# Second FFN's early u weights in tiles of their own, a scaling moved to ScalarE, and S5 output tables built in the latents' S5 projection

## The chip, the cores and the metric

The kernel runs on one core of a Trainium2 chip. The metric is the device time of one execution in microseconds (us), as the median of several executions; less is better. Engines: PE is TensorE, PEld its weight load, DVE is VectorE, ACT is ScalarE, POOL is GpSimd, SP is SyncE, whose queue issues nearly all of the DMAs here.

## What is computed

One layer of a diffusion backbone over 1024 latent tokens of width 1024, with 256 context tokens beside them, all in float32:

```
x   = x   + 0.5*gate *rms_norm((silu(g)*u) @ w_down)     # first FFN, g,u = split(h @ w_gu)
ctx = the same FFN on the context tokens
p   = modulate(rms_norm(x)) @ w_in -> bg, cg, v, u       # context: only u
y_conv = bg * grid_short_conv(cg * v)
states = S5 scan of u in both directions, from the context's last states
y_ssm  = gelu(Re(C states) + d*u), times a sigmoid gate (GLU)
x   = x + mod * rms_norm(concat(y_conv, y_ssm) @ w_out)
x   = x + 0.5*gate2*rms_norm((silu(g)*u) @ w_down2)      # second FFN
```

The FFN's inner width is 2816. Here h is the normed, modulated input. Every S5 group of 16 channels has 64 complex states; 8 neighbouring tokens form one step of the scan, so that powers 0 to 8 of the state's multiplier and tables made from them and from B and C are needed.

## The kernel before

**Stages, in order of time in the profile.** First FFN on the latents, up projection (`g_lat`, to about 540 us), first FFN on the context (`g_ctx`, to about 705 us), the down projections of both (`d_ctx`, `d_lat`, to about 1005 us), the latents' and the context's S5 input projections (`u_lat`, `u_ctx`, to about 1075 us), the S5 pairs beside the conv branch (`s5_pair`, `conv`, to about 1250 us), the output projection with the GLU (to about 1380 us), the second FFN's up projection (`g_lat` again, to about 1875 us) and its down projection.

**Matmuls.** A product is made of three passes on a high and a low half (fp32r) of both operands; `split` makes the halves with a ScalarE copy and a VectorE subtraction. The latents' FFN uses Strassen's scheme of seven products m = 1 to 7 for each of 22 feature tiles f. The first 16 products of `g_lat` (the list `early`: m = 1, 2, 5, 3 for f = 0 to 3) are an exception: they multiply raw float32, which the profile shows as two passes per matmul, 8 for a product, so that they need no halves. For m = 1 and 2 the operand is a slice of the g weights, for m = 5 it is u0+u1, for m = 3 it is g1-(u0+u1-g0); `prep` makes these on VectorE, one and three operations of 128x512.

**Weights.** Weight tiles of 512 KB pass through four buffers `wr0` to `wr3`. At build time `g_lat` simulates which tile sits in which buffer and writes a list `loads`; an entry is issued (`fetch`) once the last use of its buffer's previous tile has been emitted. With g and u of four feature tiles there are eight tiles for four buffers, so that in the second FFN u tiles replace g tiles, and g tiles come back:

```
slots, loads = [None] * 4, []
...
if n == len(early) and not apart_u:
    slots = [None] * 4
```

With `apart_u=True`, which the first FFN's call passes and the second's does not, the u tiles that the early products need are loaded by `u_load` into tiles of the pool z (32 buffers of 512 KB, shared by nearly everything), the four g tiles stay in their buffers, and the slots are not emptied after the early products.

**Order.** The framework's scheduler orders the instructions of each engine at build time: by priority (order of emission) among those that its simulation holds to be ready, and it gives out pool buffers in the same way. In the first FFN's start the program fixes the order on VectorE and TensorE (`G0`), later not. `S2` is the order in which hop steps (`h`: transposed, modulated input blocks, their Strassen sums and halves) and products (`p`) are emitted at the second FFN's start. Its m = 6 sums overwrite the tiles that m = 5's raw products read; the m = 3 products read the tiles that m = 6 frees.

**S5 tables.** `s5_prep` runs as filler of `g_ctx` (`step(FC)`, two filler steps for each feature tile). Its last loop makes the output tables, columns `CO` of `pd` in DRAM: for 4 blocks of 8 groups, six operations of 128x1024 each (24 in all), those of odd blocks on POOL and of even blocks on VectorE, and two stores of 512 KB for each block on SP's queue. `s5_pair` loads its rows of `pd` (`self.load(pa, self.pd[a, :, :EO])`) one pair ahead; the first such load is behind `u_ctx`.

**Projections.** `u_lat` is called for two halves and yields ten times in all; between its steps `run` advances `ctx_in`, the norm of the context.

Of the kernel before, what the change touches and what calls it, by code (L numbers as in the profile page):

```python
# [16 lines left out]
P = 128  # L17
D = 1024
# [8 lines left out]
H = 16  # L27
T8 = 8
# [40 lines left out]
class Kernel:  # L69
# [111 lines left out]
    def setup(self):  # L181
        nc, i = self.nc, self.i
        self.cp = self.pool("cp")
        self.dr = self.pool("dr", space=bass.MemoryType.DRAM)
        self.psum = self.pool("psum", bufs=8, space=bass.MemoryType.PSUM)
        self.sm = self.pool("sm", bufs=8)
        self.wp = self.pool("wp", bufs=6)
        self.tp = self.pool("tp", bufs=1)
        self.tb = self.t(self.tp, [P, 5 * D], "tb")
        self.ring([self.tb[:, D * k : D * k + D] for k in range(5)])  # L190
        self.wrs = [self.t(self.wp, [P, D], f"wr{k}", bufs=1) for k in range(4)]
        self.zp = self.pool("zp", bufs=32)

        dr = self.dr
        self.x1d = self.t(dr, [T8, CL, D], "x1d")
        self.x2d = self.t(dr, [T8, CL, D], "x2d")
        self.rowd = [self.t(dr, [KT, P], f"rowd{k}") for k in range(4)]
        self.pd = self.t(dr, [PAIRS, P, TO], "pd")
        self.pwd = self.t(dr, [P, D], "pwd")
        self.brd = self.t(dr, [P, D], "brd")  # L200
        self.gd = self.t(dr, [H, G, 15, H], "gd")
        self.td = self.t(dr, [P, G, P], "td")
        self.ud = self.t(dr, [G * H, T8, CL], "ud")
        self.ucd = self.t(dr, [G * H, T8, CC], "ucd")
        self.yd = self.t(dr, [T8, H, G, CL], "yd")
        self.zd = [self.t(dr, [P, NT], f"zd{k}") for k in range(4)]
        self.t1d = [self.t(dr, [P, 512], f"t1d{k}") for k in range(NF // 2)]
        self.t2d = [self.t(dr, [P, 512], f"t2d{k}") for k in range(NF // 2)]
        self.scd = [self.t(dr, [P, 4 * NC], f"scd{k}") for k in range(6)]
        self.sd = [[self.t(dr, [P, NT], f"sd{n}_{k}") for k in range(NF)] for n in range(2)]  # L210

        cp = self.cp
        rows = self.t2([16, P])
        self.load(rows[0:8, :], i["c"][0].rearrange("(k p) -> k p", p=P))
        self.load(rows[8:16, :], i["c_ctx"].rearrange("(k p) -> k p", p=P))
        self.ident = self.t(cp, [P, P], "ident")
        make_identity(self.tc.nc, self.ident)
        srow = self.t2([16, P])
        nc.scalar.activation(srow, rows, AF.Silu)
        pt = self.ps()  # L220
        self.tr(pt[:, :16], srow, 16)
        self.scol = self.t(cp, [P, 16], "scol")
        nc.vector.tensor_copy(self.scol, pt[:, :16])
        self.srep = self.t(cp, [P, KT, 32], "srep")
        nc.scalar.activation(
            self.srep.rearrange("p k (n c) -> p n c k", c=2),
            pt[:, :16].rearrange("p (c k) -> p c k", c=2).unsqueeze(1).to_broadcast([P, 16, 2, KT]), AF.Copy,
        )
        self.ones = self.t(cp, [P, 1], "ones")
        nc.gpsimd.memset(self.ones, 1.0)  # L230
        self.modc = {}
        self.mask = self.t(cp, [P, 2 * CL + 4], "mask", dt=mybir.dt.bfloat16)
        nc.gpsimd.memset(self.mask, 1.0)
        nc.gpsimd.memset(self.mask[:, :: CL + 1], 0.0)
# [1147 lines left out]
    def s5_prep(self):  # L1382
        nc, i = self.nc, self.i
        pl = nc.gpsimd
        slot = lambda shape: self.t(self.zp, shape, "z")
# [4 lines left out]
        pw, br_ = slot([P, 2, 2, T8, 32]), slot([P, 2, 32, H])  # L1390
# [4 lines left out]
        ct = slot([P, 2, 32, H])  # L1395
# [4 lines left out]
        for k in range(2):  # L1400
# [4 lines left out]
            for d in range(2):  # L1405
                r = slice(64 * d, 64 * d + 64)
# [3 lines left out]
        pdv = self.pd.rearrange("a p w -> p a w")  # L1410
        shp = [P, 8, T8, H]

        def power(w, r, gs):
            return pw[:, w, r, :, gs].rearrange("p t a -> p a t").unsqueeze(3).to_broadcast(shp)

        for o in range(4):
            gs = slice(8 * o, 8 * o + 8)
            xr, xi, xt = slot(shp), slot(shp), slot(shp)
# [38 lines left out]
        for t in range(T8):  # L1457
            r = slice(t * H, t * H + H)
# [6 lines left out]
        for t in range(T8):  # L1465
            r = slice(t * H, t * H + H)
            self.load(self.td[r], self.gd[:, :, 7 - t : 15 - t].rearrange("h g l k -> h g (l k)"))
            if t % TY == TY - 1:
                yield
        for o in range(4):  # L1470
            gs = slice(8 * o, 8 * o + 8)
            mr, mi, xt = slot(shp), slot(shp), slot(shp)
            prb, pib = power(1, 0, gs), power(1, 1, gs)
            cr_ = ct[:, 0, gs, :].unsqueeze(2).to_broadcast(shp)
            ci_ = ct[:, 1, gs, :].unsqueeze(2).to_broadcast(shp)
            e = pl if o % 2 else None
            self.mul(mr, cr_, prb, e)
            self.mul(xt, ci_, pib, e)
            self.add(mr, mr, xt, e)
            yield  # L1480
            self.mul(mi, ci_, prb, e)
            self.mul(xt, cr_, pib, e)
            self.sub(mi, mi, xt, e)
            for r, m in ((0, mr), (1, mi)):
                c0 = CO + 256 * r
                self.load(
                    pdv[:, 4 * o : 4 * o + 4, c0 : c0 + 256], m.rearrange("p (a q) t h -> p a (q t h)", q=2)
                )
            yield
# [225 lines left out]
    def run(self):  # L1715
        nc, i = self.nc, self.i
# [10 lines left out]
        hb = {m: [] for m in range(1, 8)}  # L1727
        hr = {m: [] for m in (1, 2, 5, 3)}
        xt = [self.z() for _ in range(4)]
# [8 lines left out]
        held = {f: {1: halves(tb[f])[0], 2: halves(tb[f])[1], 0: [tb[f]]} for f in range(4)}  # L1738
        held[0][5], held[0][3] = halves(tb[4])
        held[0][0].append(tb[4])  # L1740
        ffn = self.g_lat(i["ffn1_w_gu"][0], hb, hr, self.sd[0], FN, order1, 3, held, True)
# [18 lines left out]
        ab = (self.modc[1, 0], self.modc[0, 0])  # L1760
# [7 lines left out]
        bl = [self.blocks(xt, *ab), self.blocks(xt2, *ab)]  # L1768
        h = self.hops(stages, bl, hb, hr)
# [145 lines left out]
        u = self.tb.rearrange("p (g c) -> p g c", g=G)  # L1915
        cx = ctx_in()
        next(cx)
        for _ in itertools.chain(self.u_lat(mhi, mlo, 0, u), self.u_lat(mhi, mlo, 1, u)):
            next(cx, None)
        for _ in cx:  # L1920
            pass
        self.u_ctx(chi2, clo2)
# [100 lines left out]
        order2 = [(f, m) for m in (1, 2, 5, 3) for f in range(4)]  # L2023
        tb = [self.ta() for _ in range(3)]
        held = {f: {1: halves(tb[f])[0], 2: halves(tb[f])[1], 0: [tb[f]]} for f in range(3)}
        ffn = self.g_lat(i["ffn2_w_gu"][0], hb, hr, self.sd[1], (0, 0, 1, 1, 0, 1, 0), order2, 3, held)
        next(ffn)
        for _ in range(4):
            self.g_fetch()
# [10 lines left out]
        ss.append(spl(3))  # L2040
        acc = self.out_group(ss[2], wo2)
        next(p)
        ssa = self.squares(part[:4])
        for _ in range(4):
            self.g_prep()
# [15 lines left out]
        self.eager = True  # L2061
        for _ in range(4):
            self.g_prod(4, 8)
        bl[1] = self.normer(part[4:], ssa, *ab)
        for _ in range(4):
            self.g_prod(4, 99)
        act = dict(h=lambda: next(h), p=lambda: self.g_prod(4, 99))
# [106 lines left out]
```

## Time and profile before

| | |
|---|---|
| median of 3 runs (lowest to highest) | 2077.2 us (2076.4 to 2079.46) |
| the profiled execution, its span | 2077.89 us, 2076.1 us |
| mean granted TensorE clock | 0.98 |
| HBM | 282.97 MB read, 74.17 MB written |
| DMA issues for w_gu through the four buffers | 146 of 512 KB, median 4.1 us to landing |

The span is the part of the execution in which the profile has instructions; 1.8 us lie around it. In the views below all lines of the kernel read L51, the helper that records each instruction, so that groups are told apart by tile names: `ps` are PSUM banks, `wr` the raw weight buffers, `w` weight halves, `z` and `t` the two large pools.

### The profile page before, as it was taken

The page shows a single profiled execution, that of the slowest core. Times are in us where ns is not written, and L with a number is a line of the kernel's source. Part 1 is how long each engine was busy: PE and PEld are TensorE (multiplying, and loading weights), DVE is VectorE, ACT ScalarE, POOL GpSimd, SP SyncE. Part 2 cuts the span into 40 slices and gives each one's busy share as a digit, 9 for nine tenths or more (in the row PEclk, how much of TensorE's full clock was granted, in tenths as well). Part 3 has the DMA queues.
Part 4 walks back from the last instruction along what each step waited for, and adds up shares of the span by engine and source line. Part 5 has one row for each costly group of instructions (what it writes and reads, how often), then busy time and mean ns, then how long its engine had stood idle before and what let it go on. Part 6 is the DMA issues. An engine that isn't in the chain of part 4 may idle for free. (4 is left out here: it accounts for less than half of the span.)

```text
span 2076.1 us, 25812 instructions
## 1 busy us (share of the span) xinstructions
PE 1961.8 (94%) x9364; PEld 1562.7 (75%) x9364; DVE 1433.3 (69%) x2532; ACT 825.3 (40%) x1459; POOL 191.3 (9%) x106
## 2 busy tenths in 40 slices
PE   7899999989898999999998899997999999999997
PEld 3477778867898877777887778763788888887775
DVE  1874469787766679787528985486865555577977
ACT  5433333423343345566532334353333333334543
POOL 0000000040347000000003430010000000000000
PEclk9999999999999999999999999999999999999999
DMA  9167632445579977476665533134632322267554
GB/s 325 31 218 249 240 137 72 132 127 167 172 222 268 294 249 251 147 259 224 180 207 170 182 112 122 53 130 122 203 122 81 100 73 82 87 254 267 198 182 162
DMA packets 334059, 356.78 MB, mean 172 GB/s; under 512 B 47024, under 2 KB 248428, under 8 KB 333932
## 3 DMA queue, kind: packets, MB, share of 16 engines
q1 hardware_dynamic: 331628, 346.75, 51.4%
q10 hardware_dynamic: 2304, 8.39, 1.0%
q8 instruction: 73, 1.20, 0.2%
q14 instruction: 54, 0.44, 0.1%
HBM read 282.97 MB, written 74.17 MB: 172 GB/s over the span
## 5 line engine op out<-in xcount | busy, mean ns | idle before, releaser
L51 PE MATMUL ps<-z,w 128*128 128x512 f32 (+1 forms) x5328 | 1151.2, 377 | 39.6 <-DVE w L51 13.1
L51 PEld LDWEIGHTS ps<-z,w 128*128 128x128 f32 x5328 | 937.7, 192 | 236.4 <-DVE w L51 14.9
L51 PE MATMUL ps<-w,w 128*128 128x512 f32 x1848 | 427.3, 392 | 16.3 <-DVE w L51 9.7
L51 PEld LDWEIGHTS ps<-w,w 128*128 128x128 f32 x1848 | 346.4, 188 | 95.6 <-DVE w L51 14.7
L51 ACT ACTIVATE w<-wr 128x512 fp32r<-128x512 f32 (+1 forms) x270 | 206.6, 767 | 348.4 <-PE ps L51 281.7
L51 DVE TENSOR_TENSOR w<-wr,w 128x512 fp32r<-128x512 f32 (+1 forms) x264 | 246.9, 937 | 117.4 <-ACT w L51 110.8
L51 ACT ACTIVATE w<-t 128x512 fp32r<-128x512 f32 x292 | 177.1, 626 | 213.4 <-DVE t L51 129.9
L51 DVE TENSOR_TENSOR w<-t,w 128x512 fp32r<-128x512 f32 x292 | 198.6, 691 | 77.0 <-ACT w L51 76.6
L51 DVE TENSOR_TENSOR t<-t,ps 128x512 f32<-128x512 f32 x150 | 102.4, 684 | 97.6 <-PE ps L51 94.5
L51 PE MATMUL ps<-z,t 128*128 128x512 f32 x512 | 148.0, 449 | 11.4 <-DVE t L51 10.3
L51 ACT ACTIVATE t<-ps 128x512 f32<-128x512 f32 (+2 forms) x143 | 77.4, 542 | 166.3 <-PE ps L51 162.8
L51 PEld LDWEIGHTS ps<-z,t 128*128 128x128 f32 x512 | 96.8, 190 | 60.8 <-issue 36.2
L51 ACT ACTIVATE w<-z 128x512 fp32r<-128x512 f32 x110 | 69.6, 632 | 146.2 <-PE ps L51 144.0
L51 DVE TENSOR_TENSOR z<-z,z 128x512 fp32r<-128x512 f32 (+3 forms) x127 | 106.6, 869 | 15.5 <-ACT z L51 11.6
L51 DVE TENSOR_TENSOR t<-wr 128x512 f32<-128x512 f32 x140 | 94.2, 686 | 32.2 <-DMA wr<-in_ffn_w_gu 18.1
L51 ACT ACTIVATE t<-z 128x1024 bf16<-128x1024 f32 (+3 forms) x132 | 75.5, 605 | 47.2 <-DVE z L51 30.8
L51 DVE TENSOR_TENSOR w<-z,w 128x512 fp32r<-128x512 f32 x110 | 75.5, 686 | 26.6 <-ACT w L51 26.4
L51 POOL TENSOR_TENSOR z<-z,z 128x1024 f32<-128x1024 f32 x24 | 79.2, 3320 | 76.3 <-PE ps L51 42.0
L51 ACT ACTIVATE t<-t 128x512 f32<-128x512 f32 (+1 forms) x83 | 51.7, 623 | 78.6 <-DVE t L51 78.2
L51 DVE TENSOR_TENSOR z<-t,ps 128x512 f32<-128x512 f32 (+1 forms) x52 | 29.8, 573 | 64.9 <-PE ps L51 64.3
L51 POOL TENSOR_TENSOR tb<-tb 128x512 f32<-128x512 f32 x24 | 33.6, 1412 | 435.4 <-DMA sd<-z 409.0
L51 ACT ACTIVATE z<-z 128x512 fp32r<-128x512 f32 (+2 forms) x76 | 48.3, 673 | 56.7 <-DVE z L51 56.7
(121 smaller groups left out, 1402.1 us busy)
## 6 DMA issues: line engine op xcount, KB each, us to landing
wr<-in_ffn_w_gu SPq DMA_DIRECT2D x146, 512.0 KB, 4.1
wr<-in_ffn_w_down SPq DMA_DIRECT2D x198, 256.0 KB, 4.2
tb<-in_w_ada SPq DMA_DIRECT2D x56, 512.0 KB, 4.5
sd<-z SPq DMA_DIRECT2D x44, 512.0 KB, 3.0
z<-sd SPq DMA_DIRECT2D x88, 256.0 KB, 5.4
wr<-in_ffn_w_down SPq DMA_DIRECT2D x22, 512.0 KB, 4.9
wr<-in_w_in SPq DMA_DIRECT2D x20, 512.0 KB, 4.0
z<-in_w_ada SPq DMA_DIRECT2D x16, 512.0 KB, 6.3
```

What stands on the lines that cost most here:

```text
L51: r = f(*a, **kw)
```

## The change

Three parts. (1) The output tables leave `s5_prep`: it now stores the transposed C table `ct` to a new DRAM tensor `ctd`; a new generator `s5_ctab` loads the half of `pwd` with the powers and `ctd`, and makes the same four blocks, all on VectorE; `run` advances it one step after each yield of `u_lat`. (2) The second FFN's `g_lat` gets `apart_u=True`, and four `u_load` calls are put behind the second residual block's `next(p)`. (3) The scaling of the second half of the rows (`part[4:]`) by its norm runs on ScalarE; only this use of `normer` is replaced.

```diff
@@ -198,6 +198,7 @@
         self.pd = self.t(dr, [PAIRS, P, TO], "pd")
         self.pwd = self.t(dr, [P, D], "pwd")
         self.brd = self.t(dr, [P, D], "brd")
+        self.ctd = self.t(dr, [P, D], "ctd")
         self.gd = self.t(dr, [H, G, 15, H], "gd")
         self.td = self.t(dr, [P, G, P], "td")
         self.ud = self.t(dr, [G * H, T8, CL], "ud")
@@ -1467,20 +1468,30 @@
             self.load(self.td[r], self.gd[:, :, 7 - t : 15 - t].rearrange("h g l k -> h g (l k)"))
             if t % TY == TY - 1:
                 yield
+        self.load(self.ctd, ct.rearrange("p r a h -> p (r a h)"))
+
+    def s5_ctab(self):
+
+        slot = lambda shape: self.t(self.zp, shape, "z")
+        pw, ct = slot([P, 2, T8, 32]), slot([P, 2, 32, H])
+        self.load(pw.rearrange("p r t a -> p (r t a)"), self.pwd[:, 512:])
+        self.load(ct.rearrange("p r a h -> p (r a h)"), self.ctd)
+        pdv = self.pd.rearrange("a p w -> p a w")
+        shp = [P, 8, T8, H]
+        yield
         for o in range(4):
             gs = slice(8 * o, 8 * o + 8)
             mr, mi, xt = slot(shp), slot(shp), slot(shp)
-            prb, pib = power(1, 0, gs), power(1, 1, gs)
+            prb, pib = (pw[:, r, :, gs].rearrange("p t a -> p a t").unsqueeze(3).to_broadcast(shp) for r in range(2))
             cr_ = ct[:, 0, gs, :].unsqueeze(2).to_broadcast(shp)
             ci_ = ct[:, 1, gs, :].unsqueeze(2).to_broadcast(shp)
-            e = pl if o % 2 else None
-            self.mul(mr, cr_, prb, e)
-            self.mul(xt, ci_, pib, e)
-            self.add(mr, mr, xt, e)
-            yield
-            self.mul(mi, ci_, prb, e)
-            self.mul(xt, cr_, pib, e)
-            self.sub(mi, mi, xt, e)
+            self.mul(mr, cr_, prb)
+            self.mul(xt, ci_, pib)
+            self.add(mr, mr, xt)
+            yield
+            self.mul(mi, ci_, prb)
+            self.mul(xt, cr_, pib)
+            self.sub(mi, mi, xt)
             for r, m in ((0, mr), (1, mi)):
                 c0 = CO + 256 * r
                 self.load(
@@ -1915,8 +1926,12 @@
         u = self.tb.rearrange("p (g c) -> p g c", g=G)
         cx = ctx_in()
         next(cx)
+        ctab = self.s5_ctab()
         for _ in itertools.chain(self.u_lat(mhi, mlo, 0, u), self.u_lat(mhi, mlo, 1, u)):
             next(cx, None)
+            next(ctab, None)
+        for _ in ctab:
+            pass
         for _ in cx:
             pass
         self.u_ctx(chi2, clo2)
@@ -2023,7 +2038,7 @@
         order2 = [(f, m) for m in (1, 2, 5, 3) for f in range(4)]
         tb = [self.ta() for _ in range(3)]
         held = {f: {1: halves(tb[f])[0], 2: halves(tb[f])[1], 0: [tb[f]]} for f in range(3)}
-        ffn = self.g_lat(i["ffn2_w_gu"][0], hb, hr, self.sd[1], (0, 0, 1, 1, 0, 1, 0), order2, 3, held)
+        ffn = self.g_lat(i["ffn2_w_gu"][0], hb, hr, self.sd[1], (0, 0, 1, 1, 0, 1, 0), order2, 3, held, True)
         next(ffn)
         for _ in range(4):
             self.g_fetch()
@@ -2040,6 +2055,8 @@
         ss.append(spl(3))
         acc = self.out_group(ss[2], wo2)
         next(p)
+        for _ in range(4):
+            self.u_load()
         ssa = self.squares(part[:4])
         for _ in range(4):
             self.g_prep()
@@ -2061,7 +2078,8 @@
         self.eager = True
         for _ in range(4):
             self.g_prod(4, 8)
-        bl[1] = self.normer(part[4:], ssa, *ab)
+        self.scale(part[4:], self.rsq(ssa), nc.scalar)
+        bl[1] = self.blocks(part[4:], *ab)
         for _ in range(4):
             self.g_prod(4, 99)
         act = dict(h=lambda: next(h), p=lambda: self.g_prod(4, 99))
```

## Rows read from the trace of the kernel before

**Rows 1.** The page, part 1: busy time and share of each engine.

```profile
PE 1961.8 (94%) x9364; PEld 1562.7 (75%) x9364; DVE 1433.3 (69%) x2532; ACT 825.3 (40%) x1459; POOL 191.3 (9%) x106
```

**Rows 2.** Windows: length, then busy time and count by engine, PEclk, DMA share, GB/s.

```profile
640.00:700.00 60.00, 47.62 (x356) 45.90 (x355) 44.41 (x36) 17.22 (x24) 36.51 (x8) 0.91 0.91 268
...
1408.24:1456.31 48.07, 34.76 (x99) 16.33 (x97) 37.29 (x62) 17.58 (x31) 0.00 (x0) 0.92 0.38 110
1005.00:1062.00 57.00, 56.01 (x286) 46.76 (x284) 21.79 (x40) 24.74 (x46) 2.44 (x1) 1.00 0.61 177
...
1080.00:1250.00 170.00, 153.86 (x775) 130.17 (x774) 145.56 (x337) 52.13 (x117) 61.12 (x41) 0.95 0.49 163
...
1396.00:1408.24 12.24, 12.24 (x29) 5.27 (x28) 4.92 (x9) 1.89 (x3) 0.00 (x0) 1.00 0.36 112
```

**Rows 3.** Groups of instructions, 640 to 700 us: busy us, mean ns | idle before, releasers.

```profile
L51 PE MATMUL ps<-z,w 128*128 128x256 f32 x356 | 48.0, 297 | 12.4 <-ACT w L51 6.8 <-DVE w L51 5.5
...
L51 POOL TENSOR_TENSOR z<-z,z 128x1024 f32<-128x1024 f32 x8 | 36.5, 4593 | 1.2 <-DMA scd<-z 1.1
L51 DVE TENSOR_TENSOR w<-wr,w 128x1024 fp32r<-128x1024 f32 x15 | 23.4, 1578 | 8.2 <-ACT w L51 8.1
L51 DVE TENSOR_TENSOR z<-z,z 128x1024 f32<-128x1024 f32 x12 | 17.7, 1513 | 0.0
```

**Rows 4.** Timeline of PE, 667 to 693 us: start, us, instruction [idle before <-releaser].

```profile
667.32 4.42 PE L51 MATMUL ps<-z,w 128*128 128x256 f32 x24 [1.67 <-ACT w L51]
672.18 3.11 PE L51 MATMUL ps<-z,w 128*128 128x256 f32 x24 [0.45 <-DVE w L51]
678.46 14.27 PE L51 MATMUL ps<-z,w 128*128 128x256 f32 x118 [3.17 <-DVE w L51]
```

**Rows 5.** Timeline of SP's queue: start, us, DMAs issued.

```profile
649.89 5.69 SPq L51 DMA_DIRECT2D td<-gd  x8
...
656.02 4.77 SPq L51 DMA_DIRECT2D wr<-in_ffn_w_gu  x3
...
1079.77 1.00 SPq L51 DMA_DIRECT2D z<-pd  x2
```

**Rows 6.** Groups of instructions of DVE, 1005 to 1062 us.

```profile
L51 DVE TENSOR_TENSOR w<-wr,w 128x1024 fp32r<-128x1024 f32 x6 | 7.4, 1226 | 18.5 <-ACT w L51 14.4 <-PE ps L51 4.0
...
L51 DVE TENSOR_TENSOR z<-z,gate 128x1024 f32<-128x1024 f32 x1 | 1.2, 1224 | 1.6 <-ACT t L51 1.6
```

**Rows 7.** DMA issues: queue, count, size, median us to landing.

```profile
pd<-z SPq DMA_DIRECT2D x16, 512.0 KB, 3.8
...
z<-in_ffn_w_gu SPq DMA_DIRECT2D x4, 512.0 KB, 9.5
```

**Rows 8.** Timeline of PE at the second FFN's start.

```profile
1412.88 17.51 PE L51 MATMUL ps<-z,t 128*128 128x512 f32 x40 [0.98 <-DVE t L51]
...
1437.56 5.72 PE L51 MATMUL ps<-z,t 128*128 128x512 f32 x8 [7.16 <-DVE t L51]
...
1456.31 13.88 PE L51 MATMUL ps<-z,w 128*128 128x512 f32 x47 [1.61 <-DVE w L51]
```

**Rows 9.** Groups of instructions of DVE, 1408.24 to 1456.31 us.

```profile
L51 DVE TENSOR_TENSOR t<-wr 128x512 f32<-128x512 f32 x10 | 6.6, 688 | 9.5 <-DMA wr<-in_ffn_w_gu 9.5
```

**Rows 10.** The chain of waits: start, us, what.

```profile
1456.31 416.93 PE ps L51 x1783
```

**Rows 11.** Timeline of PE at the first FFN's start.

```profile
65.00 27.63 PE L51 MATMUL ps<-z,t 128*128 128x512 f32 x64
99.01 3.66 PE L51 MATMUL ps<-z,w 128*128 128x512 f32 x7 [6.37 <-ACT z L51]
103.34 14.29 PE L51 MATMUL ps<-z,w 128*128 128x512 f32 x53 [0.68 <-DVE z L51]
```

**Rows 12.** Timelines: the scaling of part[4:] on DVE, and an ACT operation of 128x1024.

```profile
1396.27 2.74 DVE L51 TENSOR_SCALAR z<-z,sy 128x1024 f32<-128x1024 f32 x4
...
1390.65 1.06 ACT L51 ACTIVATE t<-z 128x1024 bf16<-128x1024 f32 x1
```

## The prediction

> **What bounds the kernel now.** The page comes first: TensorE is busy for 94% of the span [rows 1], so time can go only where PE is idle or runs at a lower clock, and an operation moved between other engines is worth what it does to PE there. Then the windows [rows 2]. Each of the two stages that lose work holds a hole. From 640 to 700 us PE is busy for 47.6 of 60 us at a granted clock of 0.91, with DVE at 44.4 and POOL at 36.5. From 1408.24 to 1456.31 us it is busy for 34.8 of 48.1 us at 0.92, with DVE at 37.3. The projection stage, which takes the tables over, has PE busy for 56.0 of 57 us: nothing to win, but cover for other engines, since DVE works there for 21.8 us only. Third, groups and timelines of the two holes.
>
> In the first, PE waits 12.4 us in all, 5.5 for DVE's weight halves and 6.8 for ScalarE's [rows 3]. The tables are on DVE and POOL at that time: 12 DVE operations of 17.7 us, and 8 POOL operations of 36.5 us, 4.6 each. DVE's 15 weight subtractions take 1578 ns each beside them, 1226 where POOL rests [rows 3, 6]. The longest PE wait, 3.17 us, ends with such a subtraction [rows 4].
>
> In the second, PE waits 7.16 us before the sixth of the eight late early-products (m = 5 and 3) [rows 8], and DVE itself waited 9.5 us for w_gu transfers [rows 9]: u tiles can be fetched only when a g tile's last reader is through. After 1456.31 us PE runs 1783 matmuls without a wait that enters the chain [rows 10], so a gain made before it should arrive at the end.
>
> **The change, part by part.**
>
> *Tables out of the context's FFN.* This removes 24 operations and 8 stores there and adds one store of 512 KB. The waits for DVE's halves, 5.5 us, go. The clock lost behind them: 24 matmuls took 4.42 us in one place and 3.11 in the next [rows 4], 1.3 us. The waits for ScalarE, 6.8 us, I leave: they follow weight transfers issued behind eight td transfers that hold SP's queue for 5.7 us [rows 5], and these remain. Their ends are 0 (should the transfers move the stall elsewhere) and 12.4 + 1.3 = 13.7 us; I take 5.5 + 1.3 = 6.8, the part whose cause is removed. What is late next is the weight tile behind the td transfers.
>
> *Tables into the projections.* All 24 operations are now DVE's, at 1224 ns (the same shape, POOL resting [rows 6]): 29.4 us. DVE's idle time in that stage is 57.0 - 21.8 = 35.2 us [rows 2], so PE's projections cover them; with that cover gone they would cost up to 29.4. SP gets 2 loads and 8 stores, POOL loses work and nobody waits for it there. The added wait is a store's for DVE: behind it on SP stand the next weight columns of w_in and the u rows. On DVE six weight subtractions may stand behind three table operations. A block of tables needs six operations and a landed store before its buffers are free, 6 x 1.22 + 3.8 = 11.1 us [rows 7]; four blocks, 45 us, from about 1015 us end near 1060, 20 us ahead of the first pair's load at 1079.77 [rows 5]. The ends are 0 (all in idle time) and two subtractions that each wait for a three-operation step, 2 x 3.7 = 7.4 us; near the lower end, since 29.4 is less than 35.2, I take 1.5.
>
> *u tiles of their own.* No operation is added; fetches before the 9.5 us of waits go, and the four u tiles come through z buffers beforehand. The first FFN's own u tiles land 9.5 us after issue [rows 7], and here some 40 us lie between issue and use. The best case: PE never waits from 1411.9 to 1456 us, so all of 48.07 - 34.76 = 13.3 us go, and the clock stays up: 8 passes took 5.72 us where 64 take 27.63 undisturbed [rows 8, 11], 2.3 us lost; 47 matmuls took 13.88 us where the chain has 416.93 / 1783 = 0.234 each [rows 10], 2.9 us lost. Sum 18.5 us. The lower end is the first FFN, which has this very arrangement: its eight late products (64 passes) run without a gap, yet PE then waits 6.37 us [rows 11], for hop work queued on DVE. From the first of these passes to split products is 99.01 - 65.00 = 34.0 us there, 1456.31 - 1412.88 = 43.4 here [rows 8]: 9.4 better, plus the 0.98 before it, less 3.9 - 2.9 + 0.7 = 1.7 for its slower clock and second gap (60 matmuls in 17.95 us against 14.0), makes 8.7. DVE decides between the two. It has 37.3 us of work in this window. Its 16 preparations for the late products (four for m = 5, twelve for m = 3, 0.69 us each [rows 9], 11.0 us) may move ahead, as far as DVE has room before 1408 us: 12.24 - 4.92 = 7.3 us idle [rows 2], and 2.7 us that the scaling frees. That leaves 27 to 37 us, against 28 us of late products. I take the middle, 13.6: DVE's order is fixed by hand in the first FFN and free here, but it is nearly full.
>
> *Scaling on ScalarE.* Four operations of 1.06 us replace 2.74 us on DVE [rows 12]. They would end near 1400.5 instead of 1399 us, and the transposes that read them wait for PE until 1408.24: 0, hidden by the raw products; without that cover 4.2 - 2.7 = 1.5 us. On DVE it frees room for preparations, which is in the 13.6.
>
> The Trainium skill speaks against this part: "Perfetto Trace Analysis", section Optimizing Scalar/DVE Operations, says that an operation which has a fast mode on DVE is faster there, and that offloading it makes sense if DVE is saturated. By that rule, with DVE idle from 1400 to 1408 us, the sum would be 1.5 us worse; by the trace the price is hidden.
>
> **Sum.** -6.8 + 1.5 - 13.6 = -18.9 us. The profiled execution took 2077.9 us, 1.8 of it outside the span, and lies 0.7 above the median of the runs, 2077.2. That gives 2059.0 for the profiled kind and **2058.3 us** as a median.
>
> **Rivals.**
>
> *DVE limits the second FFN's start as it does in the first.* For it: DVE's 37.3 us, and [rows 11]. Against: free order there. 2077.2 - 6.8 + 1.5 - 8.7 = 2063.2 us. Chance 0.20.
>
> *The u tiles don't get ahead.* The pool's 32 buffers are full around the output projection, so that u_load waits on SP for a buffer and the change does not do what it says. For it: eight row blocks, sixteen weight and GLU tiles and four z tiles live there at once. Against: the GLU halves are released well before 1376 us. Only the tables' part is left: 2077.2 - 6.8 + 1.5 = 2071.9 us. Chance 0.10.
>
> *The tables run on into the S5 pairs: slower.* The buffers for blocks 3 and 4 come late, because the S5 inputs, the context's halves and the ring hold the rest; the table operations go on past 1079.77 us, where DVE is busy for 145.6 of 170 us [rows 2] and each operation there moves the end, 1.22 us each; the pair loads stand behind the stores on SP. All 24 would give 2077.2 - 6.8 - 8.7 + 29.4 = 2091.1 us. It decides from 13 operations on, since 13 x 1.22 = 15.9 exceeds the 15.5 gained elsewhere. Against: 20 us of slack. Chance 0.10.
>
> *The table work was hidden anyway.* The gaps from 640 to 700 us belong to weight transfers, and the second FFN lies between its two ends: 2077.2 + 1.5 - 13.6 = 2065.1 us. For it: 6.8 us of waits for ScalarE. Against: the 3.17 us gap ends on DVE. Chance 0.10.
>
> A rest of 0.05 has both gains lost in a new order of the scheduler, near 2077.
>
> **How the numbers follow.** My forecast has 0.45. A measurement of this kernel tells about 0.2%, 4.2 us, from no change, so the forecast and three rivals (0.45, 0.20, 0.10, 0.10) count as faster, less 0.02 for their upper tails; no change gets the rest of 0.05 and these tails, 0.07; slower gets 0.10. The best sum is 2077.2 - 13.7 - 18.5 = 2045.0, the worst without a slide into the pairs 2077.2 + 7.4 - 8.7 = 2075.9. The range goes from 2046 to 2074: it leaves out the slide and the rest.
>
> **What would show it.** Right: in the context's FFN no POOL operation after about 610 us and weight subtractions at 1.23 us; 24 table operations of 1.22 us on DVE between 1000 and 1060 us with PE still full; the u tiles' loads issued before 1370 us; the late early-products as one row of 64 passes in about 27.6 us, and less than 3 us of gap behind it. Wrong: table operations beyond the first pair's load, a PE wait for weight halves in the projections, a gap of some 6 us ahead of the m = 6 products, or waits for w_gu still there. If the S5 pairs' stage grows by as much as the two holes shrink, the forecast is wrong in kind.

## The result, and the profile after

The changed kernel takes **2067.17 us** as the median of 4 runs (2066.54 to 2067.38), beside 2078.14 us (2076.4 to 2079.46, 4 runs) for the kernel before: a ratio of 0.9947, 95% interval 0.993 to 0.9964, or 11.0 us. Timed again with the experiments it gave 2064.16 us beside 2076.27, ratio 0.9942 (0.9929 to 0.9956). Forecast were 2058.3 us and 18.9 us. It is faster, and inside the range that was given, but the gain is some 60% of the forecast. The profiled execution took 2066.54 us, with a span of 2064.8.

Part 1 of the page, beside [rows 1]: POOL has lost 45 us, and TensorE's work is what it was.

```profile
PE 1960.7 (95%) x9364; PEld 1561.2 (76%) x9364; DVE 1429.4 (69%) x2540; ACT 828.8 (40%) x1463; POOL 146.0 (7%) x94
```

The windows that answer to [rows 2] (length, then busy time and count by engine, PEclk, DMA share, GB/s; the third begins with the second FFN's transposes, as the one before did):

```profile
640.00:700.00 60.00, 53.13 (x416) 52.32 (x415) 24.53 (x26) 20.44 (x26) 0.00 (x0) 0.94 0.81 232
1005.00:1062.00 57.00, 53.86 (x278) 44.73 (x277) 47.58 (x63) 21.53 (x40) 2.18 (x1) 1.00 0.78 233
1406.41:1452.88 46.47, 39.02 (x122) 20.49 (x120) 41.37 (x69) 20.29 (x36) 0.00 (x0) 0.93 0.15 45
...
1080.00:1250.00 170.00, 153.53 (x773) 129.71 (x772) 145.11 (x337) 51.94 (x117) 61.15 (x41) 0.95 0.49 166
```

In the context's FFN, TensorE works 5.5 us more of 60. In the projections it works 2.2 us less of 57, while VectorE's 21.8 us have become 47.6. The second FFN's start is fuller, but VectorE is nearly full there (41.4 of 46.5 us), and the S5 pairs are as they were.

**The context's FFN.** The groups from 640 to 700 us, beside [rows 3]:

```profile
L51 PE MATMUL ps<-z,w 128*128 128x256 f32 x416 | 53.6, 292 | 6.9 <-ACT w L51 5.3 <-DVE w L51 1.5
...
L51 DVE TENSOR_TENSOR w<-wr,w 128x1024 fp32r<-128x1024 f32 x17 | 20.8, 1224 | 27.8 <-ACT w L51 27.8
```

VectorE's weight subtractions are back at 1224 ns, from 1578, and the waits for them fell from 5.5 to 1.5 us; those for ScalarE fell from 6.8 to 5.3. In [rows 3] POOL's table operations ran beside them, now none does. The Trainium skill's "GPSIMD Engine Reference", section Specifications, says that GpSimd shares its SBUF interfaces with VectorE and contends with instructions that have two SBUF inputs; the 1578 and 1224 ns agree.

What is left is one wait. TensorE's timeline, and then SP's queue, beside [rows 4, 5]:

```profile
664.71 0.50 PE L51 MATMUL ps<-z,w 128*128 128x256 f32 x2 [4.66 <-ACT w L51]
665.97 40.12 PE L51 MATMUL ps<-z,w 128*128 128x256 f32 x310 [0.76 <-DVE w L51]
```

```profile
651.28 5.76 SPq L51 DMA_DIRECT2D td<-gd  x8
657.15 12.55 SPq L51 DMA_DIRECT2D wr<-in_ffn_w_gu  x7
```

The weight tiles for it were issued behind eight td transfers, which held SP's queue for 5.76 us.

**The projections.** TensorE had 1.15 us of waits from 1000 to 1078 us (0.99 and 0.16); now its timeline shows 3.11:

```profile
1035.26 0.30 PE L51 MATMUL ps<-ident,z 128*128 128x128 f32 x1 [1.02 <-DVE z L51]
...
1051.52 1.39 PE L51 MATMUL ps<-z,w 128*128 128x256 f32 x7 [1.48 <-ACT z L51]
1053.52 8.68 PE L51 MATMUL ps<-z,w 128*128 128x256 f32 x67 [0.61 <-DVE z L51]
```

VectorE's timeline shows why: between the context norm's operations of 0.15 us stand table operations (`z<-z,z`), two at a time.

```profile
1012.80 6.91 DVE L51 TENSOR_TENSOR z<-z,z 128x1024 f32<-128x1024 f32 x6 [0.53 <-DMA z<-ctd]
...
1026.64 2.36 DVE L51 TENSOR_TENSOR z<-z,z 128x1024 f32<-128x1024 f32 x2
1028.91 0.15 DVE L51 TENSOR_TENSOR sq<-sq,sv 128x2 f32<-128x2 f32 x1
...
1055.06 1.22 DVE L51 TENSOR_TENSOR z<-z,z 128x1024 f32<-128x1024 f32 x1
```

All 24 lie between 1012.80 and 1056.3 us, 22 us ahead of the first pair's load at 1078.74.

**The second FFN's start.** TensorE's timeline, beside [rows 8]:

```profile
1378.94 27.63 PE L51 MATMUL ps<-z,wr 128*128 128x512 f32 x64
...
1409.90 17.33 PE L51 MATMUL ps<-z,t 128*128 128x512 f32 x40
1432.95 12.36 PE L51 MATMUL ps<-z,t 128*128 128x512 f32 x24 [5.72 <-DVE t L51]
...
1446.07 5.38 PE L51 MATMUL ps<-z,w 128*128 128x512 f32 x22 [0.30 <-ACT w L51]
1452.88 47.37 PE L51 MATMUL ps<-z,w 128*128 128x512 f32 x202 [1.43 <-DVE t L51]
```

The waits of 0.98, 7.16, 2.18, 1.37 and 1.61 us (13.3 in all) became 5.72, 0.30 and 1.43 (7.5). The u tiles are ahead, issued from 1309 to 1316 us, but the products still stop at the same place. VectorE's timeline has the cause:

```profile
1399.81 0.69 DVE L51 TENSOR_TENSOR tb<-tb,ps 128x512 f32<-128x512 f32 x1 [2.65 <-ACT z L51]
1403.24 0.69 DVE L51 TENSOR_TENSOR tb<-tb,ps 128x512 f32<-128x512 f32 x1 [2.74 <-PE ps L51]
1406.68 0.69 DVE L51 TENSOR_TENSOR t<-t,ps 128x512 f32<-128x512 f32 x1 [2.74 <-PE ps L51]
...
1417.09 4.29 DVE L51 TENSOR_TENSOR z<-z,z 128x512 fp32r<-128x512 f32 x7
...
1425.51 0.68 DVE L51 TENSOR_TENSOR t<-z 128x512 f32<-128x512 f32 x1
...
1432.12 0.68 DVE L51 TENSOR_TENSOR t<-wr,t 128x512 f32<-128x512 f32 x1
...
1435.74 0.68 DVE L51 TENSOR_TENSOR t<-wr,t 128x512 f32<-128x512 f32 x1
1441.22 0.69 DVE L51 TENSOR_TENSOR t<-wr 128x512 f32<-128x512 f32 x1 [4.80 <-DMA wr<-in_ffn_w_gu]
```

It stands idle for 8.1 us up to 1406.7, waiting for raw products' results; then come hop operations (`z<-z,z`), and only from 1425.5 the nine preparations for m = 3 of features 1 to 3 (`t<-z`, `t<-t,wr`, `t<-wr,t`). The one that ends at 1432.8 is what TensorE waits for at 1432.95. Only when the second and third of these features' last preparations have read their g tiles does SP issue the next two weight tiles, at 1435.28 and 1436.49, and VectorE waits 4.80 us for them.

**Where the time went, by three marks on TensorE's timeline.** The start of the first down projection (`ps<-w,w`, 128x512) closes the context's FFN; the raw products (`ps<-z,wr`) open the second FFN; the 133rd `ps<-w,w` matmul of its down projection, 33 us behind the first, is the third mark. Each row is one profiled execution; the last column is the difference of the two before it. tab_only and ffn_only have one part of the change each, no_scale has all but the scaling, and prep_early all and one edit more; they are explained below.

| kernel | context's FFN closed | raw products begin | 133rd matmul of the down projection | between the last two |
|---|---|---|---|---|
| before | 711.16 | 1380.77 | 1874.92 | 494.15 |
| ffn_only | 714.28 | 1381.27 | 1866.85 | 485.58 |
| tab_only | 706.16 | 1377.44 | 1872.53 | 495.09 |
| after | 705.93 | 1378.94 | 1864.49 | 485.55 |
| after, second time | 703.28 | 1376.36 | 1860.63 | 484.27 |
| no_scale | 706.06 | 1378.46 | 1866.57 | 488.11 |
| prep_early | 706.43 | 1378.87 | 1860.64 | 481.77 |

Kernels that are the same up to a mark differ there by 2 to 3 us, so means are taken. The five with the tables moved close the context's FFN at 705.6, the two without at 712.7: 7.1 us earlier. At the raw products they are at 1378.0 and 1381.0: 3.0 us are left, so 4.1 were given back on the way, of which the waits of the projections show about 2. The stretch between the last two marks, the second FFN's up projection and 33 us of its down projection, went from 494.6 (before, tab_only) to 485.1 us (both profiles of after, and ffn_only): 9.5 us less. Sum 12.5 us, against 11.0 and 12.1 us between the medians.

A mark carries along what lies before it. Counting TensorE's matmuls (9364 in every trace, in nearly the same order) leaves that out. From the 3200th, near 640 us, to the closing of the context's FFN it is 72.4 and 74.4 us in the two kernels with the old tables and 65.0 to 65.4 in the five: 8.1 us less. From the 5000th to the 5400th, the projections and the start of the first pair, it is 79.1 us in each of the two and 81.4 to 83.9 in the five, 3.1 more in the mean; the longer waits are 2 of these. Ahead of the 3200th matmul, and from the closing to the 5000th, TensorE has nearly the same work in all of them and single profiles differ by up to 3.3 us; there the five are 1.0 and 0.9 us slower in the mean, which is why the marks show less for the tables (3.0) than the counts (5.0).

### The profile page after: what moved, and what is told of

The parts are those of the page before. It is cut to its first block, busy times and chain, and to the rows that moved or that the text cites. A ratio compares the mean times of both kernels' runs of the same rounds, so it can differ in the third digit from the quotient of the medians.

```text
span 2064.8 us, 25793 instructions
## 1 busy us (share of the span) xinstructions
PE 1960.7 (95%) x9364; PEld 1561.2 (76%) x9364; DVE 1429.4 (69%) x2540; ACT 828.8 (40%) x1463; POOL 146.0 (7%) x94
## 5 line engine op out<-in xcount | busy, mean ns | idle before, releaser
L51 DVE TENSOR_TENSOR w<-wr,w 128x512 fp32r<-128x512 f32 (+1 forms) x264 | 239.8, 910 | 124.5 <-ACT w L51 121.8
L51 DVE TENSOR_TENSOR z<-z,z 128x512 fp32r<-128x512 f32 (+3 forms) x139 | 114.8, 859 | 15.8 <-ACT z L51 10.6
L51 DVE TENSOR_TENSOR t<-wr 128x512 f32<-128x512 f32 x132 | 89.0, 686 | 30.3 <-DMA wr<-in_ffn_w_gu 15.2
L51 DVE TENSOR_TENSOR w<-z,w 128x512 fp32r<-128x512 f32 x110 | 75.5, 686 | 20.6 <-ACT w L51 20.4
L51 PE MATMUL ps<-w,t 128*128 128x512 f32 x264 | 64.4, 401 | 1.9 <-DVE w L51 1.3
L51 POOL TENSOR_TENSOR tb<-tb 128x512 f32<-128x512 f32 x24 | 35.2, 1481 | 433.1 <-DMA sd<-z 409.6
```

Source lines behind the costliest of these rows:

```text
L51: r = f(*a, **kw)
```

## The experiments

All were timed in five rounds beside the kernel before (medians 2077.49, 2078.08 and 2076.27 us in the three groups in which they ran); ratios are to that. The first four ran together, the next four, and the last two.

**tab_only** and **ffn_only**: each part of the change alone. The edit of tab_only, to the changed kernel, takes the second FFN's part back; ffn_only is the reverse and has the tables in `s5_prep` as before.

```diff
-        ffn = self.g_lat(i["ffn2_w_gu"][0], hb, hr, self.sd[1], (0, 0, 1, 1, 0, 1, 0), order2, 3, held, True)
+        ffn = self.g_lat(i["ffn2_w_gu"][0], hb, hr, self.sd[1], (0, 0, 1, 1, 0, 1, 0), order2, 3, held)
-        for _ in range(4):
-            self.u_load()
-        self.scale(part[4:], self.rsq(ssa), nc.scalar)
-        bl[1] = self.blocks(part[4:], *ab)
+        bl[1] = self.normer(part[4:], ssa, *ab)
```

> The tables' move alone; the second FFN as in the kernel before. Theory A (what the two traces say): it won 5.2 us in the context's FFN and gave 2.4 of them back in the projections and about 0.5 behind them, so that 1.8 us are left: 2076.3 us against 2078.1, within 1.5 us. Rival B (my forecast's terms): -6.8 + 1.5 = -5.3, 2072.8 us. Under A the waits of PE in the projections (1000 to 1060 us) add up to about 3.1 us, against 1.15 before; under B they stay near 1.2.

> The second FFN's two parts alone (u tiles and scaling); the tables as in the kernel before. Theory A: 8.6 us up to the end of that FFN's up projection and about 0.9 in its down projection, together 9.2 to 9.5: 2068.8 us. Rival B: the forecast's 13.6, 2064.5 us. Rival C: the parts work on each other through the scheduler and don't add up: the sum of this run's gain and of the one with the tables alone differs from 11.0 us by more than 2.

Measured: tab_only 2074.65 us, ratio 0.9981 (0.997 to 0.9991), or 3.9 us; ffn_only 2070.45 us, 0.9967 (0.9954 to 0.998), or 6.9 us. They add up to 10.8: as far as these intervals tell, the parts don't disturb each other. tab_only lies between its two theories in time; its waits in the projections, 2.88 us, are those of theory A. ffn_only gained less in time than either of its theories has, though its stretch between the last two marks is that of after. The 5.72 us wait is there in ffn_only too (at 1435.28), so it has nothing to do with the tables, and the wait behind the td transfers is there in tab_only (4.72 us at 665.05).

**prep_early**: the last four preparations of the second FFN are emitted before the second group's steps.

```diff
+        for _ in range(4):
+            self.g_prep()
         act = dict(h=lambda: next(h), p=lambda: self.g_prod(4, 99))
```

> The changed kernel with the preparations of the four m = 3 products emitted ahead of the hop steps. Theory A: the order of DVE's work is what holds the second FFN at the low end of my bounds; the 64 late passes run as one row of 27.6 us, the 5.72 us gap goes, the next weight tiles are fetched sooner, and the time falls by 5 to 8 us, to 2059 to 2062 us. Rival B: the amount of DVE's work is the limit (37 us in that window); the gap only moves behind the late products, and the time stays within 1.5 us of 2067.2.

2061.59 us, ratio 0.992 (0.9903 to 0.9936). TensorE's timeline:

```profile
1410.96 27.73 PE L51 MATMUL ps<-z,t 128*128 128x512 f32 x64 [0.97 <-DVE z L51]
1439.12 1.25 PE L51 MATMUL ps<-z,w 128*128 128x512 f32 x4 [0.43 <-ACT w L51]
1443.44 56.89 PE L51 MATMUL ps<-z,w 128*128 128x512 f32 x237 [3.07 <-DVE w L51]
```

The 64 passes run as one row, the 5.72 us are gone, and waits of 4.47 us are left, 4.04 of them for VectorE. Between the last two marks it is 481.8 us, 3.4 less than with the change alone, and the three later kernels with this edit have 481.8 to 481.9. The time lies in theory A's range, 4.6 to 5.6 us under after, by its two ratios. So the order of VectorE's work held the 5.72 us: the same work, nine operations put ahead of hop operations, closes that gap. The idle time of VectorE up to 1406.6 us is still there (8.15 us), and all twelve preparations for m = 3 come behind it. Whether the amount of VectorE's work holds the 4.47 us that are left, as rival B says, was not tested.

**no_scale**: the change without the scaling on ScalarE.

```diff
-        self.scale(part[4:], self.rsq(ssa), nc.scalar)
-        bl[1] = self.blocks(part[4:], *ab)
+        bl[1] = self.normer(part[4:], ssa, *ab)
```

> The changed kernel with the scaling of part[4:] on VectorE again, the u tiles and the tables as changed. Theory A (the scaling is hidden on either engine: in the changed kernel its last piece is done at 1400.9 and TensorE first needs the transposed blocks at 1406.4, and VectorE stood idle for some 5.5 us just behind it): 2067.2, within 1 us. Theory B (moving it freed VectorE for the preparations that TensorE waits for): four scalings of 0.69 us come back, 2.7 us slower, 2069.9. Theory C (ScalarE is the slower engine for it, and the blocks are late by its longer time): 1.5 us faster, 2065.7.

2069.1 us, ratio 0.9955 (0.9943 to 0.9967), which overlaps with that of after, 0.9942 (0.9929 to 0.9956); the mark tells it better: 488.1 us between the last two, against 484.3 to 485.7 in five profiles of kernels whose second FFN is that of after. TensorE's timeline, then VectorE's:

```profile
1409.42 17.33 PE L51 MATMUL ps<-z,t 128*128 128x512 f32 x40
1433.63 12.09 PE L51 MATMUL ps<-z,t 128*128 128x512 f32 x24 [6.87 <-DVE t L51]
...
1454.19 46.02 PE L51 MATMUL ps<-z,w 128*128 128x512 f32 x191 [2.88 <-DVE t L51]
```

```profile
1396.12 2.74 DVE L51 TENSOR_SCALAR z<-z,sy 128x1024 f32<-128x1024 f32 x4
...
1406.20 0.69 DVE L51 TENSOR_TENSOR t<-t,ps 128x512 f32<-128x512 f32 x1 [2.75 <-PE ps L51]
...
1432.78 0.70 DVE L51 TENSOR_TENSOR t<-wr,t 128x512 f32<-128x512 f32 x1
```

Theory B has the size, 2.7 us, but not the mechanism. The four scalings go into time in which VectorE would have waited: it is at `t<-t,ps` 27.74 us after the raw products' start in both kernels (1406.20 here, 1406.68 in after). What differs is the order behind that, which the scheduler worked out anew: ahead of the preparation that TensorE waits for (`t<-wr,t` at 1432.78 and 1432.12) stand two more operations of 0.68 us, one of a hop and one for the third feature. That is 1.15 us more of wait there (6.87 against 5.72) and 1.45 at the next (2.88 against 1.43). So the scaling's place is worth about 3 us here, by the order that came with it; no run held the order and moved the scaling alone.

**tab_void**: 20 of the 24 table operations left out.

```diff
             self.mul(mr, cr_, prb)
-            self.mul(xt, ci_, pib)
-            self.add(mr, mr, xt)
             yield
-            self.mul(mi, ci_, prb)
-            self.mul(xt, cr_, pib)
-            self.sub(mi, mi, xt)
-            for r, m in ((0, mr), (1, mi)):
+            for r, m in ((0, mr), (1, mr)):
```

> The changed kernel with 20 of the 24 products and sums of the output tables left out (one product a block, written to both places of its store), so the output is not the reference's; both loads and all eight stores stay. Theory A (what the tables cost in the projections is VectorE's queue, in which the context norm's small operations and the input projections' operands stand between 1.22 us operations): TensorE's waits from 1000 to 1078 fall from 3.1 us to about 1.2 us, as before the change, and the time falls by 2 us, to 2065.2. Theory B (it is the loads and stores, or the place of the yields): the waits stay near 3 us and the time at 2067.2.

2064.61 us, ratio 0.9932 (0.9919 to 0.9944). TensorE's timeline is that of before, with the same two waits (0.99 and 0.16 us):

```profile
1049.47 7.00 PE L51 MATMUL ps<-z,w 128*128 128x256 f32 x56 [0.99 <-ACT z L51]
1056.64 30.87 PE L51 MATMUL ps<-z,w 128*128 128x256 f32 x142 [0.16 <-DVE w L51]
```

From the 5000th to the 5400th matmul it is 79.2 us, as before the change. Theory A: VectorE's queue costs the 2 us of waits; the loads and stores, which are all there, cost nothing. The raw products begin at 1375.25 us, 2.8 earlier than the mean with the tables moved.

**td_act**: the eight td transfers on ScalarE's queue. **both**: td_act and prep_early together. **both_pool**: the same, with the transfers on GpSimd's queue (`self.nc.gpsimd.dma_start` in place of `self.store`).

```diff
-            self.load(self.td[r], self.gd[:, :, 7 - t : 15 - t].rearrange("h g l k -> h g (l k)"))
+            self.store(self.td[r], self.gd[:, :, 7 - t : 15 - t].rearrange("h g l k -> h g (l k)"))
```

> The changed kernel with the eight td transfers issued from ScalarE's queue in place of SP's. Theory A: the 4.66 us wait left in the context's FFN comes from SP's queue, which issues the next weight tiles only after 5.8 us of td issues; it goes, and the time falls by 3 to 5 us, to 2062 to 2064 us. Rival B: the td transfers' own packets keep the DMA engines busy, the weight tiles land as late as before, and the time stays within 1 us of 2067.2. Rival C: ScalarE's halves of the weights wait behind the issues, and it is slower than 2068.2.

> The changed kernel with both further edits that gained when made alone: the eight stores of the block Toeplitz tiles on ScalarE's queue, and the last four preparations of the second FFN ahead of the second group's steps. Theory A (different stages, so the gains add: 5.6 and 5.5 us): 2056.1, within 1.5 us. Theory B (part of the gain of one was the clock granted to the whole run, which the other takes too): 2059 to 2061.

> The two edits together, with the eight stores of the block Toeplitz tiles on GpSimd's queue, which has no work from 593 to 1002 us in the changed kernel, in place of ScalarE's. On ScalarE their issue took 9.53 us in front of its own operand copies and left TensorE a wait of 7.01 us at 662.84. Theory A (the wait is the place behind the issuing of the stores, on whichever queue the copies or their weights stand): it goes, but for the 0.7 to 1.2 us waits that the other feature tiles have too, and the time falls by 4 to 6 us under the same kernel with ScalarE's queue, to 2053 to 2055. Theory B (the transfers themselves, 2 MB that compete with the weights, make the operands late): a wait of 4 to 7 us stays, and the time is 2059 within 1.5 us.

td_act gave 2061.72 us, ratio 0.9923 (0.9905 to 0.9942), about the time that was expected; its trace does not show the reason that was expected. A wait of 6.05 us for ScalarE stands at 659.60 in place of 4.66, which is what rival C named, and the second FFN is as in after. Its interval overlaps with that of after, and in the profile part of its lead is older than the edit: the same 15 matmuls took 2.03 us in td_act and 3.48 in both, at a place where these two kernels do not differ (TensorE's timeline of td_act, then of both). From 577 to 579 us the granted clock is 1.00 in td_act and 0.53 in both, near the lower of its two levels (1.2 and 2.4 GHz); in each of the two kernels TensorE had just run 30 small matmuls (128x32).

```profile
576.24 2.03 PE L51 MATMUL ps<-z,w 128*128 128x256 f32 x15
...
659.60 0.80 PE L51 MATMUL ps<-z,w 128*128 128x256 f32 x2 [6.05 <-ACT w L51]
```

```profile
577.05 3.48 PE L51 MATMUL ps<-z,w 128*128 128x256 f32 x15
...
662.84 0.80 PE L51 MATMUL ps<-z,w 128*128 128x256 f32 x2 [7.01 <-ACT w L51]
664.05 42.22 PE L51 MATMUL ps<-z,w 128*128 128x256 f32 x334 [0.42 <-ACT w L51]
```

both gave 2059.1 us, ratio 0.9908 (0.9895 to 0.9921), at the lower end of theory B's range and outside of theory A's: 2.5 us under prep_early, not 5.6, with overlapping intervals. In the context's FFN moving the transfers to ScalarE brought next to nothing: from the 3200th matmul to its closing both takes 64.9 us, prep_early 65.4. (td_act, with the same code there, takes 62.9.) What was gained lies in the S5 pairs and the output projection. The windows from the 5400th matmul to the raw products, of prep_early and of both:

```profile
1103.10:1378.87 275.77, 257.90 (x1224) 213.63 (x1223) 208.42 (x437) 93.93 (x195) 62.52 (x41) 0.97 0.41 133
1102.28:1375.23 272.95, 255.47 (x1223) 211.91 (x1222) 205.86 (x437) 94.00 (x195) 63.25 (x41) 0.97 0.42 134
```

All four kernels with the td transfers off SP's queue have 273.0 to 273.1 us here, the eight other profiles 275.4 to 275.9. In the four the scheduler gave VectorE's operations of this stage another order, from some 1139 us on, when the td transfers had long landed (the last at 694 us in both_pool); so 2.6 us came with that order, and not from the wait that the edit was aimed at. ScalarE's timeline of both says why that wait stayed:

```profile
652.09 9.53 ACTq L51 DMA_DIRECT2D td<-gd  x8
661.73 1.06 ACT L51 ACTIVATE w<-wr 128x1024 fp32r<-128x1024 f32 x1 [13.20 <-DMA td<-gd]
```

ScalarE, which makes the high halves of the weights, now spends 9.53 us on issuing: the wait has changed queues. In both_pool it is gone; TensorE's timeline, then POOL's:

```profile
657.54 0.51 PE L51 MATMUL ps<-z,w 128*128 128x256 f32 x2 [1.13 <-ACT w L51]
658.80 41.42 PE L51 MATMUL ps<-z,w 128*128 128x256 f32 x334 [0.76 <-DVE w L51]
```

```profile
653.25 0.81 POOL L51 DMA_DIRECT2D td<-gd  x1 [59.57 <-DMA gd<-z]
658.87 0.63 POOL L51 DMA_DIRECT2D td<-gd  x1 [4.81 <-issue]
```

The two waits of 7.43 us became 1.89, 5.5 less, and the raw products begin at 1369.68 in place of 1375.23, 5.6 earlier: theory A by the trace. On GpSimd's queue the eight also went one at a time, from 653.25 to 689.37 us, each some 0.3 us after the one before had landed, so that the queue and the transfers are not quite told apart. The larger part is the queue: the weight tile issued at 657.15 in after, behind the td transfers, is issued at 652.22 here, and it lands 5.6 us after its issue in place of 6.4. The median is 2055.71 us, ratio 0.9898 (0.9882 to 0.9914), 0.7 above theory A's range; by the ratios that is 2 us under both, with overlapping intervals, and what the marks gain more was lost again behind them (204.2 us from the third mark to the end of the span, 201.4 in both). It is the best version: 8.5 us under the changed kernel timed beside it (2064.16), 20.6 under the kernel before.

**both_tab_after**: both, but the table operations begin when the context norm has issued its own.

```diff
+        next(ctab)
         for _ in itertools.chain(self.u_lat(mhi, mlo, 0, u), self.u_lat(mhi, mlo, 1, u)):
-            next(cx, None)
-            next(ctab, None)
+            if next(cx, 1):
+                next(ctab, None)
```

> The same two edits, and the tables' operations begin only when the context norm has issued all of its own. Theory A (the norm's chain of small operations between 1.22 us table operations is what TensorE waits for near 1035): that wait of 1.0 us goes, the later ones of the projections stay, and the time is 0.5 to 1.5 us under the kernel with the two edits alone. Theory B (24 operations of 1.22 us then end too late, VectorE's operands for the last projections or the first pair's loads wait): TensorE waits more behind 1050, and it is 1 to 4 us slower than that kernel.

2079.04 us, ratio 1.0003 (0.9993 to 1.0013): 20 us slower than both, far more than either theory had. The wait near 1035 went, as theory A says, but the norm takes most of the ten steps, and what is left of the tables is emitted as one block. TensorE's timeline, then VectorE's:

```profile
1053.50 3.57 PE L51 MATMUL ps<-z,w 128*128 128x256 f32 x15 [3.77 <-DVE z L51]
1066.69 1.01 PE L51 MATMUL ps<-z,w 128*128 128x256 f32 x3 [9.62 <-ACT z L51]
1068.67 6.59 PE L51 MATMUL ps<-z,w 128*128 128x256 f32 x35 [0.97 <-DVE z L51]
```

```profile
1034.53 6.89 DVE L51 TENSOR_TENSOR z<-z,z 128x1024 f32<-128x1024 f32 x6
...
1064.79 3.50 DVE L51 TENSOR_TENSOR z<-z,z 128x1024 f32<-128x1024 f32 x3 [5.33 <-DMA pd<-z]
```

VectorE waits 5.33 us for the store that frees a table buffer, with the context's operands behind it. TensorE's waits from 1000 to 1078 us are 16.6 us instead of 3.0, its granted clock from 1040 to 1080, with these waits, is 0.74 instead of 0.96, and the raw products begin at 1392.15 us, 16.9 later than in both. It is not the prediction's slower rival: the last table operation ends at 1072.0 us, 21 us ahead of the first pair's load at 1093.57, and the time is lost within the projections.

**after_again**: the changed kernel unaltered, beside the last two.

> The changed kernel unaltered, beside the kernel before, for a narrower interval of the change itself and as the yardstick of the other runs: 2067, a ratio of 0.995 within 0.001. Under the theory that the parts measured alone add up (ratios 0.9981 and 0.9967) 0.9948; if one part disturbs the other, above 0.996.

2064.16 us, ratio 0.9942 (0.9929 to 0.9956): the ratio as expected, and beside the 0.9948 of the parts added up; the time is 3 us lower than expected.

## Why the prediction was right and where it was wrong

**What bounds the kernel**: right. Both gains came from TensorE's waits in the two stages named, and a lead at the second FFN's start arrived at the end: from the third mark on, the profiles of before and after take 201.2 and 200.3 us to the end of their spans.

**Tables out of the context's FFN, -6.8**: right. 7.1 us by the mark, 8.1 by the count of matmuls; the waits for VectorE's halves went from 5.5 to 1.5 us and the subtractions back to 1224 ns. Not all of the 5.5 us went, as the sum had it, and 1.5 of the waits for ScalarE, which it had left alone, went too. What was named as late next, the weight tile behind the td transfers, is the wait of 4.66 us that remained, and both_pool shows that it belonged in the main to the queue.

**Tables into the projections, +1.5**: the mechanism right, the size too small. The idle time of VectorE was large enough, and the slide into the S5 pairs did not come. The step that failed is the choice "near the lower end, since 29.4 is less than 35.2": idle time of a whole stage says nothing of what stands directly behind an operation. The named victims, weight subtractions, did not wait; the context norm and its blocks did. tab_void puts the price at 2 to 2.8 us, the count of matmuls at 3.1, the mark at 4.1, within the 0 to 7.4 that was given. The net of the two terms was 3.0 us by the marks, 3.9 by tab_only's ratio and 5.0 by the counts, forecast 5.3.

**u tiles, -13.6**: the step that cost most of the error. Between the ends of 8.7 (VectorE decides, as in the first FFN) and 18.5 the middle was taken, on the argument that the preparations may move ahead "as far as DVE has room before 1408 us", 7.3 us idle and 2.7 freed. The change brought 9.5 us between the marks (6.9 by ffn_only's time), close to the lower end, and by no_scale only about 6.5 of it without the scaling. The room was there, 8.1 us of idle time in the trace of after, and was not used: the four preparations for m = 5 did go ahead, but all twelve for m = 3 came after 1406.7 us, and nine of them behind hop operations. Nor was room what decided: prep_early leaves that idle time as it is, only puts the nine ahead of the hop operations, and the part gives 494.6 - 481.8 = 12.8 us, 0.8 from the forecast. So the sum of the middle can be reached, but by the order behind 1406 us and not by the idle time ahead of it, and the change as it stands did not arrange that order. The rival "DVE limits the second FFN's start as it does in the first", at 2063.2 us, describes what happened in this stage, with the order of DVE's work as the cause of the wait of 5.72 us.

**Scaling, 0**: that it is hidden was right; on ScalarE it took 4.26 us and ended at 1400.85, 5.6 us before the transposes. That it is therefore worth nothing was wrong by some 3 us, through the order of VectorE's queue. The rule from the Trainium skill's "Perfetto Trace Analysis", section Optimizing Scalar/DVE Operations, on which the sum would have been 1.5 us worse, did not decide here either: ScalarE's four operations were slower, 4.26 us against 2.74, but lay beside TensorE's raw products.

**The other rivals.** The u tiles did get ahead (issued by 1316 us). The tables' work was not hidden anyway (tab_only, 0.9981 with an interval below 1, and 8.1 us in the context's FFN). The tables did not run on into the pairs, and not in both_tab_after either; but that kernel shows that the same 24 operations, with the ten steps shared differently, cost 17 us within the projections.

**Open.** In the context's FFN td_act is 2.3 us faster than the kernels with SP's queue and both only 0.3, with one profile of each; how much is the edit can't be told. Whether the S5 pairs' other order gives its 2.6 us without moving the transfers, what the scaling's place is worth with VectorE's order held, and what holds the last 4.47 us of waits at the second FFN's start were not tested.

## What to carry to other kernels

Idle time of an engine in a stage says little of what a wait there will become: for each operation that another engine waits for, ask what is emitted ahead of it. An edit can also change the scheduler's order in a later stage, so compare every stage and not only the one that was edited. When a transfer holds up work behind its issue, look for a queue with no work in that stage; on another busy engine's queue the wait comes back in another form. And where a part is bounded by two ends, a stage of the same kernel that already has the arrangement is a better guess than the middle.

## What was not expected of the hardware

The issue of the same eight DMAs of 256 KB took 5.76 us on SP's queue and 9.53 on ScalarE's, in front of its own copies of the weights, and 0.6 to 0.8 us apiece on POOL's. The Trainium skill's "DMA: Bandwidth & Descriptors", section Issuing engines are not separate DMA queues, says that several issuing engines save only the time that a sequencer needs to start a DMA, which is usually small beside the DMA. The first half fits both_pool, where saving that time was the larger part. Apiece it is small here too, 0.7 us beside 4.4 to landing on SP's queue; but eight in a row stand in front of the next weight tile, and TensorE's waits in both_pool are 5.5 us shorter than in both.

The same 15 matmuls, in code that does not differ, took 2.03 us in some executions and 3.4 to 3.5 in others (td_act and both above), with the granted clock from 577 to 579 us at 1.00 and 0.53. So the clock alone can make single profiles differ by 1.4 us at one place, and parts of 3 us need marks of several profiles, or counts of matmuls that leave out what lies before.
